# A masked-patch loss on one core: identities ahead of the loads, target loads further forward, last columns divided over two engine paths

## Chip, cores, metric

One core of one Trainium2 chip. The metric is the device time of one execution in microseconds. "Span" is the time from the first to the last instruction in the profile of one execution; the metric is some 1.7 us more.

## The reference

```python
# pred, target: (32, 147, 768) float32; norm_pix_loss = True
mean = target.mean(axis=-1, keepdims=True)
var = target.var(axis=-1, keepdims=True)
target = (target - mean) / np.sqrt(var + 1e-6)
loss = np.mean((pred - target) ** 2, axis=-1)
return loss.mean(axis=-1)          # 32 numbers
```

## The kernel before

The 32 x 147 rows lie on 128 partitions as 36 full "columns" of 128 rows and one REST column of 96 rows, each 768 wide. One column is 0.393 MB in f32; pred and target are 28.90 MB together. Each column goes through five steps:

- VectorE takes mean and variance (two `bn_stats`, one `bn_aggr`);
- ScalarE and VectorE make 1/sqrt(var) for a group of columns;
- GpSimd normalises the column to bf16 (`s`);
- the difference pred - s is formed either on TensorE (two products with identities, accumulated in tiles in PSUM, whose size the code counts in banks; called the ACT path) or on VectorE (`difference`);
- the square with its sum along the row is taken on ScalarE or VectorE, and at the end TensorE adds the partial sums over partitions in `acc`.

The first target columns and REST are loaded as f32 by SyncE's and ScalarE's queues; all else is loaded by GpSimd's queue, which casts to bf16 on the way.

```python
    piece("t", 0, 4, q="hw")                   # SyncE's queue, f32
    piece("t", REST, REST + 1, q="hw2")        # ScalarE's queue, f32
    piece("t", 4, 8)                           # GpSimd's queue, cast to bf16
    piece("p", REST, REST + 1)
    piece("t", 8, 12)
    piece("p", 0, 4)
    ...
    piece("t", 28, 32)
    piece("p", 12, 16)
    piece("t", 32, 36)
    for c in range(16, 32, 2):
        piece("p", c, c + 2)
    for c in range(32, 35):
        piece("p", c, c + 1)
    piece("p", KM - 1, KM, 0, half)
    piece("p", KM - 1, KM, half, D)
    ...
    units = [((c, c + 1), 0, D, "ACT" if c < 18 else "DVE+ACT") for c in range(0, 24, 2)]
    units.insert(2, ((REST,), 0, D, "ACT"))
    units += [((24,), 0, D, "DVE"), ((25,), 0, D, "DVE+ACT"), ((26, 27), 0, D, "DVE+ACT")]
    units += [((c,), 0, D, "ACT" if c % 2 else "DVE") for c in range(28, KM - 1)]
    units += [((KM - 1,), 0, half, "ACT"), ((KM - 1,), half, D, "ACT")]
```

Every operation gets an assumed duration, its needs, a rank and an earliest time. A small list scheduler in the kernel's own source (not on the chip) emits them in the order in which this model would start them. On the chip each engine then works **in that order**, whether or not something behind is ready earlier (below, VectorE stands idle for 1.29 us with ready work behind).

```python
            t = max([free[engine], early] + [end[x] + (0.0 if ops[by_name[x]][1] == engine else HOP) for x in needs])
            key = (t - (1.0 if name[0] == "root" else 0.0), rank, i)
```

GpSimd has eight load slots in this kernel: its load k is issued only after its load k - 8 has landed (before: the first landed at 11.78 us, the ninth was issued at 12.06).

Of the kernel before, what the change touches and what calls it, by code (L numbers as in the profile page):

```python
# [7 lines left out]
F32 = mybir.dt.float32  # L8
# [6 lines left out]
def kernel(  # L15
# [26 lines left out]

    data = ctx.enter_context(tc.tile_pool(name="data", bufs=1))
    work = ctx.enter_context(tc.tile_pool(name="work", bufs=16))
    diffs = ctx.enter_context(tc.tile_pool(name="diffs", bufs=4))
    small = ctx.enter_context(tc.tile_pool(name="small", bufs=8))
    singles = ctx.enter_context(tc.tile_pool(name="singles", bufs=1))
    psum = ctx.enter_context(tc.tile_pool(name="psum", bufs=2, space=bass.MemoryType.PSUM))
    psum1 = ctx.enter_context(tc.tile_pool(name="psum1", bufs=1, space=bass.MemoryType.PSUM))


# [3 lines left out]
    def piece(kind, c0, c1, d0=0, d1=D, q="sw"):  # L55
        stream.append((kind, c0, c1, d0, d1, q))

    piece("t", 0, 4, q="hw")
    piece("t", REST, REST + 1, q="hw2")
    piece("t", 4, 8)  # L60
    piece("p", REST, REST + 1)
    piece("t", 8, 12)
    piece("p", 0, 4)
    piece("t", 12, 16)
    piece("t", 16, 20)
    piece("p", 4, 8)
    piece("t", 20, 24)
    piece("t", 24, 28)
    piece("p", 8, 12)
    piece("t", 28, 32)  # L70
    piece("p", 12, 16)
    piece("t", 32, 36)
    for c in range(16, 32, 2):
        piece("p", c, c + 2)
    for c in range(32, 35):
        piece("p", c, c + 1)
# [1 line left out]
    piece("p", KM - 1, KM, half, D)  # L78


    groups = [tuple(range(0, 4)), (REST,)] + [tuple(range(c, c + 4)) for c in range(4, 16, 4)]
    groups += [(c, c + 1) for c in range(16, KM, 2)]


    units = [((c, c + 1), 0, D, "ACT" if c < 18 else "DVE+ACT") for c in range(0, 24, 2)]
    units.insert(2, ((REST,), 0, D, "ACT"))
    units += [((24,), 0, D, "DVE"), ((25,), 0, D, "DVE+ACT"), ((26, 27), 0, D, "DVE+ACT")]
    units += [((c,), 0, D, "ACT" if c % 2 else "DVE") for c in range(28, KM - 1)]
    units += [((KM - 1,), 0, half, "ACT"), ((KM - 1,), half, D, "ACT")]



# [3 lines left out]
    def op(name, engine, dur, needs, fn, rank=0.0, early=0.0):  # L96
        by_name[name] = len(ops)
        ops.append((name, engine, dur, needs, fn, rank, early))
# [13 lines left out]
            KIND[kind].setdefault(c, []).append((d0, d1, til, (c - c0) * w))  # L112


    land, lanes, clock = {}, {"hw": [], "hw2": [], "sw": []}, 2.9
    for i, (kind, c0, c1, d0, d1, q) in enumerate(stream):
        w = (c1 - c0) * (d1 - d0)
        clock += w * rows_of(c0) / P * 0.915 / D + (0.0 if w >= 4 * D else 0.04)
# [7 lines left out]
    def landed(kind, c):  # L126
        return max(t for (k, cc, d), t in land.items() if k == kind and cc == c)
# [19 lines left out]
                                        base=per - 1, pattern=[[per, B]], channel_multiplier=-1))  # L147

    op("eps", "DVE", 0.1, [], lambda: pin(nc.vector.memset(eps_t, eps)))
    op("ident", "POOL", 1.6, [], identities, early=2.0)  # L150
    op("masks", "POOL", 3.0, [], masks, early=3.0)

    mvs = {}
# [9 lines left out]
    def stats(g, i):  # L163
        n, K = rows_of(g[0]), len(g)
        if i == 0:
            mvs[g] = small.tile([P, K, 2], F32, name="mv")
        if not norm_pix_loss:
            return
        (_, _, til, o), = tbuf[g[i]]
        bn(mvs[g][:n, i], [til[:n, o + a:o + a + half] for a in (0, half)])  # L170
# [20 lines left out]

    for k, g in enumerate(groups):
        for i, c in enumerate(g):
            op(("bn", c), "DVE", 1.26, [], lambda g=g, i=i: stats(g, i), rank=k - 50.0, early=landed("t", c))
        op(("root", k), "ACT", 0.55, [("bn", c) for c in g], lambda g=g: root(g), rank=-1.0)
        op(("recip", k), "DVE", 0.2, [("root", k)], lambda g=g: recip(g), rank=-60.0)

# [21 lines left out]

    def product(u, d0, w, src, so, eye, first):  # L220
        n, z = rows_of(u[0]), zs[u, d0]
        for a in range(0, w, BANK):
            b = min(w, a + BANK)
            pin(nc.tensor.matmul(z[:n, a:b], eye[:n, :n], src[:n, so + a:so + b], start=first, stop=not first))  # L224

    def sub_target(u, d0, w):
        if (u, d0) == units[-1][:2]:
            zs[u, d0] = psum1.tile([P, BANK], F32, name="z_last")
        else:
            zs[u, d0] = psum.tile([P, 3 * BANK], F32, name="z")  # L230
        s, so = sbuf[u[0]]
        product(u, d0, w, s, so + d0, nident, True)

# [7 lines left out]
    def difference(u, d0, w):  # L241

        z = zs[u, d0] = diffs.tile([P, 2 * D], BF16, name="zd")
        s, so = sbuf[u[0]]
        til, o = pred_of(u[0], d0)
        pin(nc.vector.tensor_tensor(out=z[:, :w], in0=til[:, o:o + w], in1=s[:, so + d0:so + d0 + w],  # L246
                                    op=ALU.subtract))

    def square_dve(u, d0, w, dest):
        z = zs[u, d0][:, :w]  # L250
        pin(nc.vector.scalar_tensor_tensor(out=z, in0=z, scalar=1.0, in1=z, op0=ALU.mult, op1=ALU.mult,  # L251
                                           accum_out=dest))

    tail = 5
    n_early = len(units) - 1 - tail
    rl = singles.tile([P, n_early], F32)
    rl_sum = singles.tile([P, 1], F32)
    finals = []
    early_ops, users, seen = [], [], set()
    for k, (u, d0, d1, eng) in enumerate(units):  # L260
        w = len(u) * D if len(u) > 1 else d1 - d0
        arrive = max(t for (kk, c, d), t in land.items() if kk == "p" and c in u and d < d1)
        norms = [("norm", c) for c in u]
        for c in u:
# [11 lines left out]
            dest = singles.tile([P, 1], F32, name=f"rl{k}")  # L276
            finals.append((("sq", k), dest, mask, P))
        if eng in ("DVE", "DVE+ACT"):
            op(("diff", k), "DVE", 0.57 * w / D + 0.05, norms, lambda u=u, d0=d0, w=w: difference(u, d0, w), rank=-2.0,
               early=arrive)  # L280
            if eng == "DVE":
                op(("sq", k), "DVE", 1.0 * w / D, [("diff", k)],
                   lambda u=u, d0=d0, w=w, dest=dest: square_dve(u, d0, w, dest), rank=-1.0)
            else:
                op(("sq", k), "ACT", 0.75 * w / D + 0.25, [("diff", k)],
                   lambda u=u, d0=d0, w=w, dest=dest: square_act(u, d0, w, dest), rank=k)
            continue
        op(("subt", k), "PE", 0.37 * w / D, norms + (users[-2:-1] if k < len(units) - 1 else []) + ["ident"],
           lambda u=u, d0=d0, w=w: sub_target(u, d0, w), rank=k + 0.0)
        op(("pred", k), "PE", 0.37 * w / D, [("subt", k)], lambda u=u, d0=d0, w=w: add_pred(u, d0, w), rank=k,  # L290
           early=arrive)
        op(("sq", k), "ACT", 0.73 * w / D + 0.23, [("pred", k)],
           lambda u=u, d0=d0, w=w, dest=dest: square_act(u, d0, w, dest), rank=k)
        users.append(("sq", k))

    acc = psum1.tile([1, B], F32)
    def early_sum():
        junk = singles.tile([P, n_early], F32, name="junk")
        pin(nc.scalar.activation(out=junk, in_=rl, func=ACTF.Copy, accum_out=rl_sum))

    op("rl_sum", "ACT", 0.4, early_ops, early_sum, rank=50.0)
    finals.insert(0, ("rl_sum", rl_sum, mask, P))
    turn = []

    def final(vec, m, n):
        turn.append(n)
        pin(nc.tensor.matmul(acc, vec[:n], m[:n], start=len(turn) == 1, stop=len(turn) == len(finals)))  # L307

    for i, (need, vec, m, n) in enumerate(finals):
        op(("final", i), "PE", 0.2, [need, "masks"], lambda v=vec, m=m, n=n: final(v, m, n), rank=90.0)  # L310


    HOP = 0.15
# [59 lines left out]
```

## Time and profile before

| | before |
|---|---|
| time, median | 77.22 us (3 runs, 77.22 to 77.61) |
| span | 75.4 us |
| first data packet / last landing | 2.20 / 71.50 us |
| copy of the result to SBUF, then its transfer | 73.26 us |
| busy: VectorE, GpSimd, ScalarE, TensorE | 75, 72, 42, 40% |

The prediction shows the page's lines for these. How to read them: in the 40-slice rows a digit is the busy share of one slice in tenths. In a window's row each engine has its busy time and (x instructions), and the last three columns are TensorE's granted clock, DMA share and GB/s written. In a timeline's row stand start, duration, engine, line, operation and tiles, and in brackets how long the engine had been idle and who released it. "Landing" is the last of the completion records of a load.

### The profile page before, as it was taken

The page shows a single profiled execution, that of the slowest core. Times are in us where ns is not written, and L with a number is a line of the kernel's source. Part 1 is how long each engine was busy: PE and PEld are TensorE (multiplying, and loading weights), DVE is VectorE, ACT ScalarE, POOL GpSimd, SP SyncE. Part 2 cuts the span into 40 slices and gives each one's busy share as a digit, 9 for nine tenths or more (in the row PEclk, how much of TensorE's full clock was granted, in tenths as well). Part 3 has the DMA queues.
Part 4 walks back from the last instruction along what each step waited for, and adds up shares of the span by engine and source line. Part 5 has one row for each costly group of instructions (what it writes and reads, how often), then busy time and mean ns, then how long its engine had stood idle before and what let it go on. Part 6 is the DMA issues. An engine that isn't in the chain of part 4 may idle for free.

```text
span 75.4 us, 570 instructions
## 1 busy us (share of the span) xinstructions
PE 30.3 (40%) x87; PEld 8.7 (11%) x88; DVE 56.3 (75%) x148; ACT 32.0 (42%) x73; POOL 54.4 (72%) x77
## 2 busy tenths in 40 slices
PE   0000000038596540688700778287544000348860
PEld 0000000001232110211100211031111000112220
DVE  0000099999999999976999928960999989989940
ACT  1400000210229802289210297239366099799550
POOL 4998205099999999499989898999878799800000
PEclk9999999999999997555555557965995555555555
DMA  0899999999999999999999999999999999999700
GB/s 0 215 424 339 262 192 236 218 209 215 212 215 215 212 216 225 212 209 215 215 212 215 219 212 225 209 212 202 214 215 209 215 210 210 214 205 205 117 0 0
DMA packets 3973, 15.41 MB, mean 204 GB/s; under 512 B 450, under 2 KB 1186, under 8 KB 3842
## 3 DMA queue, kind: packets, MB, share of 16 engines
q0 software_dynamic: 3712, 13.52, 89.2%
q1 hardware_dynamic: 146, 1.57, 5.7%
q10 hardware_dynamic: 112, 0.29, 1.0%
q14 instruction: 3, 0.02, 0.1%
HBM read 28.90 MB, written 0.00 MB: 383 GB/s over the span
## 4 chain that ended last, share of the span: by engine, by line
DMA 60%; DVE 18%; POOL 9%; issue 6%; PE 2%; ACT 1%; POOLq 0%; ACTq 0%
DMA t<-in_target_dram 49%; DVE st L160 14%; DMA p<-in_pred_dram 11%; POOL s L210 8%; DVE mv L161 3%; DVE zd L246 1%; PE acc L307 1%; POOL t L110 1%; PE z L224 1%; ACT z_last L239 1%; PE z_last L224 1%; POOLq L368 0%; DVE r L190 0%; POOL p L110 0%; DVE ob L336 0%
## 5 line engine op out<-in xcount | busy, mean ns | idle before, releaser
L160 DVE BATCH_NORM_STATS2 st<-t 128x6 f32<-128x384 bf16 (+2 forms) x74 | 36.3, 532 | 11.6 <-DMA t<-in_target_dram 11.6
L210 POOL TENSOR_SCALAR s<-t,nm,r 128x768 bf16<-128x768 bf16 (+2 forms) x37 | 38.2, 1040 | 3.2 <-ACT nm L185 2.0
L224 PE MATMUL z<-s,nident 128*128 128x512 bf16 (+4 forms) x36 | 14.6, 511 | 23.3 <-POOL s L210 17.6
L239 ACT ACTIVATE z<-z 128x1536 f32<-128x1536 f32 (+3 forms) x14 | 16.6, 1184 | 6.9 <-PE z L224 6.8
L224 PE MATMUL z<-p,ident 128*128 128x512 bf16 (+4 forms) x35 | 14.2, 542 | 12.1 <-DMA p<-in_pred_dram 12.0
L184 ACT ACTIVATE r<-mv,eps_t 128x2 f32<-128x2 f32 (+2 forms) x15 | 4.4, 293 | 29.5 <-DVE mv L161 28.8
L110 POOL DMA_DIRECT2D p<-in_pred_dram x18 | 10.2, 565 | 2.7 <-DVE st L160 1.0
L246 DVE TENSOR_TENSOR zd<-p,s 128x768 bf16<-128x768 bf16 (+1 forms) x10 | 9.7, 991 | 0.5 <-ACT zd L239 0.3
L161 DVE BATCH_NORM_AGGREGATE mv<-st 128x2 f32<-128x12 f32 (+1 forms) x37 | 7.7, 209 | 1.3
L110 POOL DMA_DIRECT2D t<-in_target_dram x8 | 4.9, 628 | 4.7 <-DMA t<-in_target_dram 3.9
L239 ACT ACTIVATE zd<-zd 128x1536 bf16<-128x1536 bf16 (+1 forms) x5 | 6.7, 1345 | 2.7 <-DVE zd L246 2.7
L224 PEld LDWEIGHTS <-ident 128*128 128x128 bf16 (+1 forms) x37 | 4.7, 126 | 27.2 <-issue 26.2
L224 PEld LDWEIGHTS <-nident 128*128 128x128 bf16 (+1 forms) x37 | 3.4, 114 | 34.6 <-issue 14.4
L251 DVE SCALAR_TENSOR_TENSOR zd<-zd 128x768 bf16<-128x768 bf16 x5 | 4.8, 955 | 0.1
L224 PE MATMUL z_last<-s,nident 128*128 128x384 bf16 x1 | 0.5, 479 | 7.1 <-POOL s L210 7.1
L190 DVE RECIPROCAL r<-r 128x2 f32<-128x2 f32 (+2 forms) x15 | 1.9, 123 | 1.7 <-ACT r L184 1.7
L185 ACT ACTIVATE nm<-mv 128x2 f32<-128x2 f32 (+2 forms) x15 | 2.8, 188 | 0.0
L239 ACT ACTIVATION_READ_ACCUMULATOR z<-z 128x1 f32 (+1 forms) x14 | 2.7, 190 | 0.0
L184 ACT ACT_TABLE_LOAD x1 | 1.3, 1283 | 1.5 <-PEq L354 1.5
L307 PE MATMUL acc<-mask,rl 128*1 128x32 f32 x10 | 1.0, 224 | 0.4 <-ACT z_last L239 0.4
L239 ACT ACTIVATION_READ_ACCUMULATOR zd<-zd 128x1 f32 x5 | 0.9, 187 | 0.0
L336 DVE COPY ob<-acc 1x32 f32<-1x32 f32 x1 | 0.2, 178 | 1.0 <-PE acc L307 1.0
(26 smaller groups left out, 5.8 us busy)
## 6 DMA issues: line engine op xcount, KB each, us to landing
t<-in_target_dram POOLq DMA_DIRECT2D x8, 768.0 KB, 24.5
p<-in_pred_dram POOLq DMA_DIRECT2D x4, 768.0 KB, 27.4
p<-in_pred_dram POOLq DMA_DIRECT2D x8, 384.0 KB, 20.9
t<-in_target_dram SPq DMA_DIRECT2D x1, 1536.0 KB, 8.4
p<-in_pred_dram POOLq DMA_DIRECT2D x3, 192.0 KB, 12.7
t<-in_target_dram ACTq DMA_DIRECT2D x1, 288.0 KB, 9.6
p<-in_pred_dram POOLq DMA_DIRECT2D x2, 96.0 KB, 7.3
p<-in_pred_dram POOLq DMA_DIRECT2D x1, 144.0 KB, 10.4
```

The costliest lines, as they stand in the source:

```text
L110: pin(eng.dma_start(out=til[:n], in_=src))
L160: pin(nc.vector.bn_stats(out=st[:n, j, :], in_=x))
L161: pin(nc.vector.bn_aggr(out=out, in_=st[:n, :len(parts)]))
L184: pin(nc.scalar.activation(out=r[:n], in_=mv[:n, :, 1], func=ACTF.Sqrt, bias=eps_t[:n], scale=1.0))
L185: pin(nc.scalar.activation(out=nm[:n], in_=mv[:n, :, 0], func=ACTF.Copy, scale=-1.0))
L190: pin(nc.vector.reciprocal(out=rs[g][:n], in_=rs[g][:n]))
L210: pin(nc.gpsimd.tensor_scalar(out=s[:n, so:so + D], in0=til[:n, o:o + D], scalar1=nm, scalar2=r, op0=ALU.add, op1=ALU.mult))
L224: pin(nc.tensor.matmul(z[:n, a:b], eye[:n, :n], src[:n, so + a:so + b], start=first, stop=not first))
L239: pin(nc.scalar.activation(out=z[:n, :w], in_=z[:n, :w], func=ACTF.Square, accum_out=dest[:n]))
L246: pin(nc.vector.tensor_tensor(out=z[:, :w], in0=til[:, o:o + w], in1=s[:, so + d0:so + d0 + w], op=ALU.subtract))
L251: pin(nc.vector.scalar_tensor_tensor(out=z, in0=z, scalar=1.0, in1=z, op0=ALU.mult, op1=ALU.mult, accum_out=dest))
L307: pin(nc.tensor.matmul(acc, vec[:n], m[:n], start=len(turn) == 1, stop=len(turn) == len(finals)))
```

## The change

The intent is to make the identities while no data are there yet, to let target run further ahead of pred so that statistics and normalisation are done earlier, to make groups and pieces of four columns, and to divide the last columns so that ScalarE and VectorE each take a part of every one.

```diff
+    piece("t", 8, 12)
     piece("p", REST, REST + 1)
-    piece("t", 8, 12)
+    piece("t", 12, 16)
     piece("p", 0, 4)
-    piece("t", 12, 16)
 ... (each target piece moved forward likewise)
     piece("p", 8, 12)
-    piece("t", 28, 32)
-    piece("p", 12, 16)
     piece("t", 32, 36)
-    for c in range(16, 32, 2):
+    for c in range(12, 24, 4):
+        piece("p", c, c + 4)
+    for c in range(24, 32, 2):
         piece("p", c, c + 2)
 ...
+    groups = [(0, 1), (2, 3), (REST,)] + [tuple(range(c, c + 4)) for c in range(4, KM, 4)]
+    units = [((c, c + 1), 0, D, "ACT" if c < 14 else "DVE+ACT") for c in range(0, 24, 2)]
+    units += [((24,), 0, D, "DVE"), ((25,), 0, D, "DVE+ACT")]
+    for u in [(c, c + 1) for c in range(26, KM - 4, 2)] + [(c,) for c in range(KM - 4, KM - 1)]:
+        m = BANK if u[0] < KM - 2 else half
+        units += [(u, 0, m, "ACT"), (u, m, D, "DVE")]
+    units += [((KM - 1,), 0, half, "ACT"), ((KM - 1,), half, D, "DVE")]
 ...
-    op("ident", "POOL", 1.6, [], identities, early=2.0)
+    op("ident", "POOL", 1.3, [], identities, rank=-2.0)
 ...
-            op(("bn", c), ..., rank=k - 50.0, early=landed("t", c))
+            op(("bn", c), ..., rank=k - 50.0 if c < 32 or c == REST else -1.5, early=landed("t", c))
```

With it come two pools of accumulators in turn (two of three banks for the pairs, then three of two banks, `zp`, for the tail), five difference buffers for four, the sum of the early parts on VectorE instead of ScalarE, and new durations in the scheduler's model. The REST column was on ScalarE's queue already, so that part of the description changes nothing.

More of the change, by code (lines that the diff above doesn't have):

```diff
@@ L44 @@
     work = ctx.enter_context(tc.tile_pool(name="work", bufs=16))
-    diffs = ctx.enter_context(tc.tile_pool(name="diffs", bufs=4))
+    diffs = ctx.enter_context(tc.tile_pool(name="diffs", bufs=5))
     small = ctx.enter_context(tc.tile_pool(name="small", bufs=8))
     singles = ctx.enter_context(tc.tile_pool(name="singles", bufs=1))
-    psum = ctx.enter_context(tc.tile_pool(name="psum", bufs=2, space=bass.MemoryType.PSUM))
     psum1 = ctx.enter_context(tc.tile_pool(name="psum1", bufs=1, space=bass.MemoryType.PSUM))
@@ L60 @@
     piece("t", 4, 8)
+    piece("t", 8, 12)
     piece("p", REST, REST + 1)
-    piece("t", 8, 12)
+    piece("t", 12, 16)
     piece("p", 0, 4)
-    piece("t", 12, 16)
     piece("t", 16, 20)
+    piece("t", 20, 24)
     piece("p", 4, 8)
-    piece("t", 20, 24)
     piece("t", 24, 28)
+    piece("t", 28, 32)
     piece("p", 8, 12)
-    piece("t", 28, 32)
-    piece("p", 12, 16)
     piece("t", 32, 36)
-    for c in range(16, 32, 2):
+    for c in range(12, 24, 4):
+        piece("p", c, c + 4)
+    for c in range(24, 32, 2):
         piece("p", c, c + 2)
@@ L78 @@
     piece("p", KM - 1, KM, half, D)
-    groups = [tuple(range(0, 4)), (REST,)] + [tuple(range(c, c + 4)) for c in range(4, 16, 4)]
-    groups += [(c, c + 1) for c in range(16, KM, 2)]
-    units = [((c, c + 1), 0, D, "ACT" if c < 18 else "DVE+ACT") for c in range(0, 24, 2)]
+    groups = [(0, 1), (2, 3), (REST,)] + [tuple(range(c, c + 4)) for c in range(4, KM, 4)]
+    units = [((c, c + 1), 0, D, "ACT" if c < 14 else "DVE+ACT") for c in range(0, 24, 2)]
     units.insert(2, ((REST,), 0, D, "ACT"))
-    units += [((24,), 0, D, "DVE"), ((25,), 0, D, "DVE+ACT"), ((26, 27), 0, D, "DVE+ACT")]
-    units += [((c,), 0, D, "ACT" if c % 2 else "DVE") for c in range(28, KM - 1)]
-    units += [((KM - 1,), 0, half, "ACT"), ((KM - 1,), half, D, "ACT")]
+    units += [((24,), 0, D, "DVE"), ((25,), 0, D, "DVE+ACT")]
[3 more added lines that the diff above has]
+    units += [((KM - 1,), 0, half, "ACT"), ((KM - 1,), half, D, "DVE")]
     ops, by_name = [], {}
@@ L112, in load @@
             KIND[kind].setdefault(c, []).append((d0, d1, til, (c - c0) * w))
-    land, lanes, clock = {}, {"hw": [], "hw2": [], "sw": []}, 2.9
+    land, lanes, clock = {}, {"hw": [], "hw2": [], "sw": []}, 2.3
     for i, (kind, c0, c1, d0, d1, q) in enumerate(stream):
@@ L193 @@
         for i, c in enumerate(g):
-            op(("bn", c), "DVE", 1.26, [], lambda g=g, i=i: stats(g, i), rank=k - 50.0, early=landed("t", c))
+            op(("bn", c), "DVE", 1.26, [], lambda g=g, i=i: stats(g, i), rank=k - 50.0 if c < 32 or c == REST else -1.5, early=landed("t", c))
         op(("root", k), "ACT", 0.55, [("bn", c) for c in g], lambda g=g: root(g), rank=-1.0)
@@ L221, in product @@
         n, z = rows_of(u[0]), zs[u, d0]
-        for a in range(0, w, BANK):
-            b = min(w, a + BANK)
-            pin(nc.tensor.matmul(z[:n, a:b], eye[:n, :n], src[:n, so + a:so + b], start=first, stop=not first))
+        runs = [(0, so, w)] if w % D == 0 else [(k * BANK, so + k * D, w // len(u)) for k in range(len(u))]
+        for zo, o, e in runs:
+            for a in range(0, e, BANK):
+                b = min(e, a + BANK)
+                pin(nc.tensor.matmul(z[:n, zo + a:zo + b], eye[:n, :n], src[:n, o + a:o + b],
+                                     start=first, stop=not first))
     def sub_target(u, d0, w):
-        if (u, d0) == units[-1][:2]:
-            zs[u, d0] = psum1.tile([P, BANK], F32, name="z_last")
-        else:
-            zs[u, d0] = psum.tile([P, 3 * BANK], F32, name="z")
+        if u in pairs_pe:
+            zs[u, d0] = pools["pairs"].tile([P, 3 * BANK], F32, name="z")
+            pairs_pe.remove(u)
+        else:
+            if "parts" not in pools:
+                pools["stack"].close()
+                pools["parts"] = ctx.enter_context(tc.tile_pool(name="parts", bufs=3, space=bass.MemoryType.PSUM))
+            zs[u, d0] = pools["parts"].tile([P, 2 * BANK], F32, name="zp")
         s, so = sbuf[u[0]]
@@ L245, in difference @@
         til, o = pred_of(u[0], d0)
-        pin(nc.vector.tensor_tensor(out=z[:, :w], in0=til[:, o:o + w], in1=s[:, so + d0:so + d0 + w],
-                                    op=ALU.subtract))
+        K, e = len(u), w // len(u)
+        if e == D:
+            x, y, v = z[:, :w], til[:, o:o + w], s[:, so:so + w]
+        elif K == 1:
+            x, y, v = z[:, :w], til[:, o:o + w], s[:, so + d0:so + d0 + w]
+        else:
+            x = z[:, :w].rearrange("p (k d) -> p k d", d=e)
+            y = til[:, o - d0:o - d0 + K * D].rearrange("p (k d) -> p k d", d=D)[:, :, d0:d0 + e]
+            v = s[:, so:so + K * D].rearrange("p (k d) -> p k d", d=D)[:, :, d0:d0 + e]
+        pin(nc.vector.tensor_tensor(out=x, in0=y, in1=v, op=ALU.subtract))
     def square_dve(u, d0, w, dest):
@@ L252, in square_dve @@
                                            accum_out=dest))
-    tail = 5
+    tail = 6
     n_early = len(units) - 1 - tail
@@ L257 @@
     rl_sum = singles.tile([P, 1], F32)
+    pairs_pe = [u for u, d0, d1, eng in units if eng == "ACT" and (u[0] == REST or len(u) * (d1 - d0) > 2 * BANK)]
+    n_pairs = len(pairs_pe)
+    pools = {"stack": ExitStack()}
+    pools["pairs"] = pools["stack"].enter_context(tc.tile_pool(name="psum", bufs=2, space=bass.MemoryType.PSUM))
     finals = []
-    early_ops, users, seen = [], [], set()
+    early_ops, users, dusers, dprev, seen = [], [], [], [], set()
     for k, (u, d0, d1, eng) in enumerate(units):
-        w = len(u) * D if len(u) > 1 else d1 - d0
+        w = len(u) * (d1 - d0)
         arrive = max(t for (kk, c, d), t in land.items() if kk == "p" and c in u and d < d1)
@@ L278 @@
         if eng in ("DVE", "DVE+ACT"):
-            op(("diff", k), "DVE", 0.57 * w / D + 0.05, norms, lambda u=u, d0=d0, w=w: difference(u, d0, w), rank=-2.0,
+            op(("diff", k), "DVE", 0.57 * w / D + 0.05, norms + dusers[-5:-4] + dprev[-1:], lambda u=u, d0=d0, w=w: difference(u, d0, w), rank=-2.0,
                early=arrive)
+            dusers.append(("sq", k))
+            dprev.append(("diff", k))
             if eng == "DVE":
@@ L284 @@
             else:
-                op(("sq", k), "ACT", 0.75 * w / D + 0.25, [("diff", k)],
+                op(("sq", k), "ACT", 0.65 * w / D + 0.22, [("diff", k)],
                    lambda u=u, d0=d0, w=w, dest=dest: square_act(u, d0, w, dest), rank=k)
             continue
-        op(("subt", k), "PE", 0.37 * w / D, norms + (users[-2:-1] if k < len(units) - 1 else []) + ["ident"],
+        op(("subt", k), "PE", 0.37 * w / D, norms + (users[-2:-1] if len(users) < n_pairs else users[n_pairs - 1:n_pairs] + users[n_pairs:][-3:-2]) + ["ident"],
            lambda u=u, d0=d0, w=w: sub_target(u, d0, w), rank=k + 0.0)
@@ L291 @@
            early=arrive)
-        op(("sq", k), "ACT", 0.73 * w / D + 0.23, [("pred", k)],
+        op(("sq", k), "ACT", 0.65 * w / D + 0.22, [("pred", k)],
            lambda u=u, d0=d0, w=w, dest=dest: square_act(u, d0, w, dest), rank=k)
@@ L296 @@
     acc = psum1.tile([1, B], F32)
-    def early_sum():
-        junk = singles.tile([P, n_early], F32, name="junk")
-        pin(nc.scalar.activation(out=junk, in_=rl, func=ACTF.Copy, accum_out=rl_sum))
-    op("rl_sum", "ACT", 0.4, early_ops, early_sum, rank=50.0)
+    op("rl_sum", "DVE", 0.2, early_ops, lambda: pin(nc.vector.tensor_reduce(
+        out=rl_sum, in_=rl, axis=mybir.AxisListType.X, op=ALU.add)), rank=-3.0)
     finals.insert(0, ("rl_sum", rl_sum, mask, P))
@@ L309 @@
     for i, (need, vec, m, n) in enumerate(finals):
-        op(("final", i), "PE", 0.2, [need, "masks"], lambda v=vec, m=m, n=n: final(v, m, n), rank=90.0)
+        op(("final", i), "PE", 0.2, [need, "masks"], lambda v=vec, m=m, n=n: final(v, m, n), rank=90.0,
+           early=max(land.values()) + 0.4)
     HOP = 0.15
```

## The prediction

> **What bounds the kernel now.** I read the page first: the slices of part 2 (is anything full all the time?), then part 4 (the chain that ended last), then windows and timelines of the first 12 us and the last 15 us. From the page:
>
> ```profile
> span 75.4 us, 570 instructions
> PE 30.3 (40%) x87; PEld 8.7 (11%) x88; DVE 56.3 (75%) x148; ACT 32.0 (42%) x73; POOL 54.4 (72%) x77
> ...
> DMA  0899999999999999999999999999999999999700
> GB/s 0 215 424 339 262 192 236 218 209 215 212 215 215 212 216 225 212 209 215 215 212 215 219 212 225 209 212 202 214 215 209 215 210 210 214 205 205 117 0 0
> ...
> DMA 60%; DVE 18%; POOL 9%; issue 6%; PE 2%; ACT 1%; POOLq 0%; ACTq 0%
> ```
>
> The reader is to see that no engine is full but the transfers are: the DMA row holds a 9 from slice 2 (3.8 us) to slice 36 (69.7 us). The kernel reads 28.90 MB, a fixed amount, and the loads by GpSimd write half of what they read (f32 to bf16), so 215 GB/s written is 430 GB/s read. The windows of the stretches give the rates:
>
> ```profile
> 12.00:40.00 28.00, 13.60 (x36) 3.85 (x36) 26.20 (x79) 10.10 (x28) 24.18 (x29) 0.81 1.04 215
> 52.00:60.00 8.00, 3.40 (x10) 0.83 (x9) 7.17 (x15) 3.81 (x9) 6.92 (x9) 0.71 1.07 210
> 60.00:66.00 6.00, 0.66 (x2) 0.21 (x2) 5.77 (x10) 5.33 (x8) 5.26 (x4) 0.50 1.08 212
> 66.00:70.00 4.00, 2.75 (x8) 0.91 (x7) 3.63 (x9) 3.61 (x8) 0.00 (x0) 0.50 1.12 204
> ```
>
> The last two columns are DMA share and GB/s: full everywhere, 2% slower with two-column pieces (from about 52 us), 5% with the smallest at the end. So the time has three parts: a head until the engines are full (first data packet at 2.20 us by the packet records, full from 3.5 us), a body of transfers until the last piece has landed (71.50 us by the landing records; the piece before it 71.00), and a tail of 3.9 us to the end of the span. The tail, from the timeline:
>
> ```profile
> 71.05 0.48 PE L224 MATMUL z<-p,ident 128*128 128x384 bf16 x1 [0.26 <-DMA p<-in_pred_dram]
> 71.30 0.96 DVE L251 SCALAR_TENSOR_TENSOR zd<-zd 128x768 bf16<-128x768 bf16 x1
> ...
> 71.78 0.50 PE L224 MATMUL z_last<-p,ident 128*128 128x384 bf16 x1
> ...
> 72.32 0.47 ACT L239 ACTIVATE z_last<-z_last 128x384 f32<-128x384 f32 x1 [0.18 <-PE z_last L224]
> 72.71 0.19 ACT L239 ACTIVATION_READ_ACCUMULATOR z_last<-z_last 128x1 f32 x1
> ...
> 72.96 0.26 PE L307 MATMUL acc<-mask,rl 128*1 128x32 f32 x2 [0.37 <-ACT z_last L239]
> 73.26 0.18 DVE L336 COPY ob<-acc 1x32 f32<-1x32 f32 x1 [0.99 <-PE acc L307]
> ```
>
> The last half column (z_last) lands at 71.50, but PE is busy with accumulations until 71.78, then PE, ScalarE and PE again: its sum is ready at 72.90. VectorE is nearly as late: its square of column 34 ends at 72.26. From the copy to the end of the span there are 2.1 us (the output's transfer), which nothing here changes.
>
> **What the Trainium skill says.** "DMA: Bandwidth & Descriptors", section "Where 436 GB/s comes from", puts the ceiling of a core's ports at 435 GB/s; the trace agrees, 430 GB/s read in the body. So nothing that makes an engine faster can shorten the body. The same page, section "Issuing engines are not separate DMA queues", says that loads issued by different engines interleave on the same 16 DMA engines; the trace agrees: from 5 to 8 us packets of all three queues alternate. Its specifications give about 1 us to the first byte of a GpSimd load; the trace differs: GpSimd issues its first at 1.32 and its first packet moves at 5.78, 4.46 us later, behind the f32 load. "GPSIMD Engine Reference", section "Key points", says that GpSimd shares its SBUF interfaces with VectorE, with contention for VectorE instructions with two SBUF inputs. The trace shows it: the difference zd<-p,s of 1536 elements takes 0.90 to 0.95 us where two ran back to back, but 2.69 us at 57.45 while GpSimd normalises, and a normalisation (0.98 usually) takes 2.29 us at 60.42 during two differences.
>
> **The change part by part.**
> (a) Identities first. In the timeline they run at 5.64 to 6.93, 1.29 us. Ahead of the loads they put GpSimd's first issue off by 0.8 to 1.3 us (to 2.1 to 2.6), and by the same 4.46 us its first packet to 6.6 to 7.05. Do the DMA engines run dry? By 5.5 us 93 of the 128 big f32 packets and 13 of the 96 of the REST column have started. Left are 35 x 0.473 + 83 x 0.121 = 26.6 us of one engine, / 16 = 1.66 us, so that work lasts until 7.16. Just enough: cost 0, at worst 0.3 us. In return the first four target columns no longer share with GpSimd's load and land some 1.2 us earlier (before: 9.23).
> (b) The REST column on ScalarE's queue: the kernel before already loads it so. Nothing.
> (c) Target further forward. Columns 32 to 35 are behind 49.5 columns of stream, not 53.5; a column costs 0.916 us here (0.393 MB / 0.429), so they land 3.7 us earlier: 49.1 for 52.80. Their statistics (1.13 us a column on VectorE, from the chain: 0.90 + 0.21 + 0.02) end at about 53.5 for 57.3, and GpSimd's last normalisation near 59 for 65.2. It moves no bytes and so no end of the body by itself: it makes slack for VectorE's last 15 us.
> (d) Pred 16 to 24 in pieces of four columns: 3.15 MB at 429 rather than 420 GB/s, 7.33 for 7.50 us: the body ends 0.17 us earlier, last landing 71.33. Two issues fewer on GpSimd (0.56 each) lie beside.
> (e) Groups of four for root: 11 for 15, four times 0.48 us off ScalarE and 0.12 off VectorE, beside.
> (f) Pairs 14 and 16 to the VectorE path: +2 x 0.95 us there. The later units are split: VectorE gets 512 columns of each pair 26, 28, 30, 256 of 32 and 33, 384 of 34 and 35. With 0.145 + w/1920 us for a difference (0.545 at 768), 0.157 + w/960 for the square (0.957 at 768) and 0.08 for the sum's read: 1.18, 0.78 and 0.98 us. Five pair differences 4.7, column 24 1.6, column 25 0.55, three pairs 3.5, two columns 1.6, two halves 2.0: 13.9 us between 53.5 and the end, where it has 17.8 until 71.33. Up to 4 us of contention with GpSimd's last four normalisations still fit, so VectorE should keep up with the landings.
> (g) The end. Second half of 35 lands at 71.33; difference 0.35, square 0.56, read 0.08: 72.35. First half lands at 70.83; PE 0.48, then ScalarE, which is finishing 34 until 71.45: + 0.58 = 72.05. ScalarE backwards: pair 30 lands 67.47, two products 0.86, square of 1024 at 1.0 + 0.1, then 0.68 each for 32 and 33 and 0.6 for 34; that fits. So the last partial sum is there at 72.35 for 72.90: 0.55 us, of which 0.17 are of (d).
> Sum: 0 (a, most likely) - 0.55 (d and g) = 76.67; with a little of (a)'s risk, 76.7 us.
>
> **The rivals.** (1) A hole at the start: GpSimd's loads come 1.3 us later, and every idle us of the DMA engines is a us of the time. For it: the margin in (a) is 0.1 to 0.5 us. Against: 4.46 us is probably partly a wait behind f32 packets, which would not grow. It would give 76.9 to 77.3. (2) VectorE as the bound at the end: it was back to back from 57 to 72 and gets more differences, which lock against GpSimd. For it: the 2.69 us above. Against: 3.7 us of head start. If it ended 1 us late, 77.5. (3) Everything is hidden: body and output transfer are the same, and the gain of the split is eaten by accumulations on PE (eight now, seven before) or by ScalarE: 77.2, no difference. (4) A larger gain would need a shorter body; the only idle capacity is the ramp from 2.2 to 3.5 us (0.7 us at most), and no part touches it.
>
> **Range and chances.** The certain parts are small: 67 of 77 us are bytes at the ceiling. From 76.2 (all gains and a cleaner start) to 77.3 (hole at the start, tail as before). Faster by over 2% means below 75.68, 1.5 us, nearly all of the tail that is not output: chance 0.05. Slower by over 2%, above 78.8, needs a hole over 1.5 us or VectorE 2 us late: 0.03. Within 2%: 0.92.
>
> **What would show it.** (a) right: the identities at about 1 us, first GpSimd packets at 6.6 to 7.1, no slice under 9 in slices 2 to 4, first landing near 8. (c) right: the last statistics end near 53.5, GpSimd's last normalisation before 61. (d) right: the last landing at 71.3 +- 0.3. (g) right: the last VectorE square within 1.1 us of that landing and the last accumulation near 72.4. I am wrong if a slice of the DMA row dips, if the last square starts more than 0.3 us behind its difference, or if the chain at the end runs back through VectorE or GpSimd rather than to the landing.

## The result and the profile after

The changed kernel took **77.03 us** (median of 6 runs, 76.89 to 77.14) against 77.24 us for the kernel before (6 runs): ratio 0.9962, 95% interval 0.9942 to 0.9983. The difference is small and real, and the verdict at 2% is "same".

The page of the changed kernel, its span, engines, transfers and chain:

```profile
span 75.3 us, 551 instructions
PE 30.0 (40%) x81; PEld 8.8 (12%) x82; DVE 56.2 (75%) x155; ACT 30.4 (40%) x65; POOL 53.5 (71%) x75
...
DMA  0899999999999999999999999999999999999700
...
DMA 40%; DVE 34%; POOL 12%; ACT 3%; PE 3%; issue 3%; ACTq 0%; POOLq 0%
```

The DMA row is the same, digit for digit. The chain is put together differently in the middle, but the end of the body is not: the last landing is at 71.54 us, for 71.50 before. What moved is the tail, in the changed kernel's timeline:

```profile
71.63 0.36 DVE L265 TENSOR_TENSOR zd<-p,s 128x384 bf16<-128x384 bf16 x1
...
72.03 0.56 DVE L269 SCALAR_TENSOR_TENSOR zd<-zd 128x384 bf16<-128x384 bf16 x1
72.11 0.48 ACT L249 ACTIVATE zp<-zp 128x384 f32<-128x384 f32 x1
72.51 0.08 DVE L269 DVE_READ_ACCUMULATOR zd<-zd 128x1 f32 x1
72.51 0.19 ACT L249 ACTIVATION_READ_ACCUMULATOR zp<-zp 128x1 f32 x1
...
73.16 0.18 DVE L359 COPY ob<-acc 1x32 f32<-1x32 f32 x1 [0.57 <-PE acc L328]
```

The two halves of column 35 now end side by side, VectorE's at 72.59 and ScalarE's at 72.70, where ScalarE's last ended at 72.90. The copy comes 1.62 us after the last landing instead of 1.76.

The rest of the profile shows that the forward order worked only half. Target 32 to 36 landed at 49.27, for 52.80. But VectorE's timeline of the changed kernel has this:

```profile
51.54 0.21 DVE L162 BATCH_NORM_AGGREGATE mv<-st 128x2 f32<-128x12 f32 x1
53.04 0.96 DVE L265 TENSOR_TENSOR zd<-p,s 128x1536 bf16<-128x1536 bf16 x1 [1.29 <-DMA p<-in_pred_dram]
53.91 1.01 DVE L161 BATCH_NORM_STATS2 st<-t 128x6 f32<-128x384 bf16 x2
```

After two of the last four columns VectorE stands idle for 1.29 us in front of a difference whose pred has not landed, with the statistics of columns 34 and 35 ready behind it. The scheduler's model had that pred landed by then and put the difference first: of operations that could start at the same time the lower rank goes first, and here -2.0 stands against -1.5, the rank that this change itself gave to the last statistics. So the statistics ended at 56.3 us and GpSimd's last normalisation at 65.5, no earlier than before (65.2).

### The profile page after: what moved, and what is told of

It is laid out like the page before. It is cut to its first block, busy times and chain, and to the rows that moved or that the text cites. A ratio compares the mean times of both kernels' runs of the same rounds, so it can differ in the third digit from the quotient of the medians. Undisturbed runs are those within 1.5% of the kernel's fastest.

```text
span 75.3 us, 551 instructions
## 1 busy us (share of the span) xinstructions
PE 30.0 (40%) x81; PEld 8.8 (12%) x82; DVE 56.2 (75%) x155; ACT 30.4 (40%) x65; POOL 53.5 (71%) x75
## 4 chain that ended last, share of the span: by engine, by line
DMA 40%; DVE 34%; POOL 12%; ACT 3%; PE 3%; issue 3%; ACTq 0%; POOLq 0%
DMA p<-in_pred_dram 29%; DVE st L161 28%; DMA t<-in_target_dram 11%; POOL s L211 11%; DVE mv L162 6%; ACT zp L249 3%; PE zp L228 3%; POOL p L111 1%; PE acc L328 1%; DVE r L191 0%; ACTq L391 0%; DVE ob L359 0%; ACTq L249 0%; POOLq L211 0%
## 5 line engine op out<-in xcount | busy, mean ns | idle before, releaser
L228 PE MATMUL z<-p,ident 128*128 128x512 bf16 (+2 forms) x23 | 10.4, 616 | 17.6 <-DMA p<-in_pred_dram 17.6
L228 PE MATMUL z<-s,nident 128*128 128x512 bf16 (+2 forms) x23 | 10.1, 563 | 16.6 <-POOL s L211 15.4
L249 ACT ACTIVATE z<-z 128x1536 f32<-128x1536 f32 (+1 forms) x8 | 10.9, 1357 | 10.6 <-PE z L228 10.6
L185 ACT ACTIVATE r<-mv,eps_t 128x4 f32<-128x4 f32 (+2 forms) x11 | 3.2, 292 | 27.7 <-DVE mv L162 27.0
L265 DVE TENSOR_TENSOR zd<-p,s 128x1536 bf16<-128x1536 bf16 (+4 forms) x14 | 9.6, 700 | 3.6 <-DMA p<-in_pred_dram 3.5
L228 PE MATMUL zp<-p,ident 128*128 128x512 bf16 (+1 forms) x9 | 4.7, 594 | 6.9 <-DMA p<-in_pred_dram 6.9
L249 ACT ACTIVATE zp<-zp 128x1024 f32<-128x1024 f32 (+2 forms) x7 | 5.1, 735 | 1.8 <-PE zp L228 1.8
L228 PE MATMUL zp<-s,nident 128*128 128x512 bf16 (+1 forms) x10 | 5.0, 607 | 2.0 <-ACT z L249 1.7
L269 DVE SCALAR_TENSOR_TENSOR zd<-zd 128x512 bf16<-128x512 bf16 (+3 forms) x8 | 5.0, 623 | 0.2
L186 ACT ACTIVATE nm<-mv 128x4 f32<-128x4 f32 (+2 forms) x11 | 2.1, 190 | 0.0
```

The lines of the kernel that those rows point to most:

```text
L185: pin(nc.scalar.activation(out=r[:n], in_=mv[:n, :, 1], func=ACTF.Sqrt, bias=eps_t[:n], scale=1.0))
L186: pin(nc.scalar.activation(out=nm[:n], in_=mv[:n, :, 0], func=ACTF.Copy, scale=-1.0))
L228: pin(nc.tensor.matmul(z[:n, zo + a:zo + b], eye[:n, :n], src[:n, o + a:o + b], start=first, stop=not first))
L249: pin(nc.scalar.activation(out=z[:n, :w], in_=z[:n, :w], func=ACTF.Square, accum_out=dest[:n]))
L265: pin(nc.vector.tensor_tensor(out=x, in0=y, in1=v, op=ALU.subtract))
L269: pin(nc.vector.scalar_tensor_tensor(out=z, in0=z, scalar=1.0, in1=z, op0=ALU.mult, op1=ALU.mult, accum_out=dest))
```

## The experiments

The theory after the result: bytes set the end of the body, the gain is the shorter tail, and part of the predicted tail was lost to a wait for an accumulator. The rivals: a poorer start through the identities; the order of the loads as the true source, through VectorE's head start; differences that are only scatter. Kernels are compared only within the same rounds.

| run | median us (range) | ratio to before, 95% | last landing | landing to copy |
|---|---|---|---|---|
| changed kernel | 77.03 (76.89 to 77.14) | 0.9962 (0.9942, 0.9983) | 71.54 | 1.62 |
| own_banks | 76.88 (76.73 to 77.09) | 0.9966 (0.9954, 0.9978) | 71.60 | 1.41 |
| ident_back | 76.90 (76.74 to 76.96) | 0.9964 (0.9952, 0.9976) | 71.43 | 1.62 |
| two_col | 77.44 (76.94 to 77.65) | 1.0031 (1.0007, 1.0056) | 71.52 | 2.03 |
| tail_only | 77.14 (76.96 to 77.53) | 1.0005 (0.9986, 1.0024) | 71.63 | 1.60 |
| after_again | 76.95 (76.75 to 77.14) | 0.9975 (0.9959, 0.9992) | 71.43 | 1.51 |
| own_banks2 | 76.89 (76.78 to 77.11) | 0.9972 (0.9958, 0.9986) | 71.41 | 1.50 |
| best | 77.02 (76.95 to 77.10) | 0.9985 (0.9973, 0.9997) | 71.46 | 1.67 |
| order_back | 78.28 (78.02 to 78.38) | 1.0143 (1.0126, 1.0160) | 71.35 | 2.80 |
| before_again | 77.21 (1 run) | - | 71.58 | 1.75 |
| masks_first | 77.10 (77.06 to 77.34) | 0.9984 (0.9970, 0.9997) | 71.95 | 1.52 |
| order_back_stats | 76.87 (76.60 to 77.02) | 0.9950 (0.9933, 0.9968) | 71.52 | 1.36 |
| no_p12 (wrong) | 74.77 (74.73 to 74.87) | 0.9685 (0.9670, 0.9700) | 67.89 | 3.05 |

Each row has 4 to 6 executions, before_again one. The kernel before had medians of 77.15, 77.11 and 77.23 us in the three calls. The last two columns are from one profile each. Two profiles of one kernel differ by up to 0.18 us in the landing and up to 0.12 us in the stretch to the copy, which is the limit of what can be read from them.

### own_banks and own_banks2: the wait for an accumulator

In the changed kernel's timeline TensorE, at 69.96 us, starts the product for column 34 only when ScalarE has freed an accumulator, and the ready product of column 33 stands behind it. ScalarE is then idle for 0.48 us.

```profile
69.96 0.50 PE L228 MATMUL zp<-s,nident 128*128 128x384 bf16 x1 [0.35 <-ACT zp L249]
...
70.99 0.58 ACT L249 ACTIVATE zp<-zp 128x512 f32<-128x512 f32 x1 [0.48 <-PE zp L228]
```

```diff
-                pools["parts"] = ctx.enter_context(tc.tile_pool(name="parts", bufs=3, ...))
-            zs[u, d0] = pools["parts"].tile([P, 2 * BANK], F32, name="zp")
+                for nb, bufs in ((2, 2), (1, 3)):      # 2 tiles of two banks, 3 of one bank
+                    pools[nb] = ctx.enter_context(tc.tile_pool(name=f"parts{nb}", bufs=bufs, ...))
+            zs[u, d0] = pools[len(u)].tile([P, len(u) * BANK], F32, name=...)
 (and the needs of the products in the scheduler's model to match)
```

> The changed kernel, but the accumulator tiles of the tail are two of two banks (pairs 26, 28, 30) and three of one bank (columns 32, 33, 34, first half of 35) instead of three of two banks. Theory (the predicted 0.55 us shrank because TensorE, in order, held the ready product of column 33 behind the product of column 34, which waited until 69.96 us for a free accumulator): ScalarE's idle 0.48 us before 70.99 goes, its last square ends near 72.2 for 72.70, VectorE's last sum (72.59) becomes the last one, the copy of the result moves from 73.16 to about 72.95, time 0.15 to 0.25 us below the changed kernel's 77.03: 76.8 to 76.9. Rival (the landing and VectorE alone set the end): no change, 77.03 within 0.07.

> The kernel with the accumulator tiles of one bank for the single columns, a second time, now beside the changed kernel. Theory (TensorE held ScalarE up by a wait for an accumulator): copy 1.4 us after the last landing instead of 1.6, time 0.15 to 0.25 us below after_again of the same rounds. Rival (times differ by where the last landing falls, and the tail's 0.2 us are within that scatter): no difference clear of the interval.

The wait of 0.48 us went, though in own_banks2 a later one of 0.31 us took part of its place: ScalarE's last sum came 0.69 us (own_banks) and 1.05 us (own_banks2) after the last landing, instead of 1.16 and 1.14 in the two profiles of the changed kernel. The time did not follow. Beside the changed kernel on one chip it was 76.89 against 76.95, ratios 0.9972 against 0.9975, the same. VectorE's last sum, at 72.65 and 72.47 us, had taken over. The wait was real and worth nothing measurable, so the theory that it had eaten a measurable part of the gain fell.

### ident_back: identities behind the loads

```diff
-    op("ident", "POOL", 1.3, [], identities, rank=-2.0)
+    op("ident", "POOL", 1.6, [], identities, early=2.0)
```

> The changed kernel with the identities back behind the first eight loads of GpSimd. Theory (the engines never run dry at the start, so the identities' place is free): first GpSimd packet back from 5.97 to 5.78 us, last landing unchanged at 71.54 within 0.1, time 77.03 within 0.08. Rival (the later loads cost a hole or a poorer start, which hides the gain of the larger pieces): last landing 0.15 to 0.2 us earlier, time 76.85.

The first GpSimd packet moved back to 5.69 us, the last landing was 71.43 (the changed kernel: 71.54 and 71.43), and the ratio 0.9964 is between the changed kernel's 0.9962 and 0.9975. The place of the identities is worth nothing that these runs can measure, in either direction.

### masks_first: how much later may GpSimd's loads start?

```diff
-    op("masks", "POOL", 3.0, [], masks, early=3.0)
+    op("masks", "POOL", 1.5, [], masks, rank=-2.0)
```

> The changed kernel with the masks ahead of the loads of GpSimd as well, so that its first load is issued near 3.1 us instead of 1.83. Theory (the first GpSimd packet waits behind f32 packets already queued, so it moves by less than the issue does, and the engines do not run dry before 7.2 us): first packet at 6.3 to 6.9 us, DMA share full throughout, last landing within 0.1 us of 71.5, time within 0.1 us of the changed kernel, 76.85 to 77.05. Rival (a fixed 4.1 us from issue to packet): first packet at 7.2 us, some hole, time 0.1 to 0.3 us more, 77.1 to 77.3.

The timeline of this run, GpSimd alone, shows the first load behind both:

```profile
1.60 0.29 POOL L139 TENSOR_SCALAR_AFFINE_SELECT nident<-nident 128x128 bf16<-128x128 bf16 x1
...
2.93 0.21 POOL L147 TENSOR_SCALAR_AFFINE_SELECT mask_rest<-mask_rest 96x32 f32<-96x32 f32 x1
3.08 1.24 POOL L111 DMA_DIRECT2D t<-in_target_dram  x2
```

The first packet came at 7.16 us, 4.08 after the issue, as the rival said. In the ten profiles with an issue at 1.83 us or later it came 3.9 to 4.2 us after the issue; in the four with an issue at 1.32 it came 4.4 to 4.6 us after, at 5.69 to 5.87, so something held those. What, is open. The first four target columns landed at 8.90 us (9.08 to 9.33 in the profiles with an issue at 1.83 or 1.84): the mechanism of the prediction's step (a) exists, but it needs a later GpSimd load.

The rival's hole is there too. While the first packet was awaited, the DMA share fell, here from 6 to 7.2 us beside the same stretch of the changed kernel (second row):

```profile
6.00:7.20 1.20, 0.00 (x0) 0.00 (x0) 0.00 (x0) 0.00 (x0) 1.20 (x3) 1.00 0.87 300
```

```profile
6.00:7.20 1.20, 0.00 (x0) 0.00 (x0) 0.00 (x0) 0.00 (x0) 0.99 (x6) 1.00 0.98 317
```

That is 0.13 us of 16 engines. What it cost in time is not settled. The last landing of this profile (71.95) is 0.4 to 0.5 us later than the changed kernel's, but the profiled execution was the slowest of the six (77.34 us; the other five took 77.06 to 77.13). The ratio 0.9984 is 0.1 to 0.2% above the changed kernel's two, and its interval overlaps both of theirs.

### two_col: pieces of two columns for pred 16 to 24

```diff
-    for c in range(12, 24, 4):
-        piece("p", c, c + 4)
-    for c in range(24, 32, 2):
+    piece("p", 12, 16)
+    for c in range(16, 32, 2):
         piece("p", c, c + 2)
```

> The changed kernel with pred 16 to 24 in four pieces of two columns, as before the change. Theory (the larger pieces do save what the packet times say, and something else in the body took it back): the 8 columns take 7.48 instead of 7.35 us, last landing 0.13 to 0.17 us later, time 77.15 to 77.2. Rival (the size of the pieces is worth nothing): 77.03 within 0.07.

The eight columns took 7.42 us (landings 52.83 to 60.25) instead of 7.35, and the last landing was 71.52. So the pieces are worth 0.07 us here (0.13 between the first profiles of before and after, 7.48 to 7.35). Yet the kernel was slower than expected and scattered over 0.7 us. The reason was elsewhere, in its timeline:

```profile
65.19 2.72 DVE L268 SCALAR_TENSOR_TENSOR zd<-zd 128x512 bf16<-128x512 bf16 x1
```

```profile
65.44 1.94 POOL L210 TENSOR_SCALAR s<-t,nm,r 128x768 bf16<-128x768 bf16 x2
```

This square takes 0.69 us elsewhere. It lasted through both of GpSimd's last normalisations, and VectorE carried the delay to the end: its last sum came at 73.23, for 72.59. Why these normalisations ran so late is in VectorE's timeline before that:

```profile
56.82 1.53 DVE L264 TENSOR_TENSOR zd<-p,s 128x1536 bf16<-128x1536 bf16 x1
58.28 1.00 DVE L160 BATCH_NORM_STATS2 st<-t 128x6 f32<-128x384 bf16 x2
...
60.56 0.18 DVE L190 RECIPROCAL r<-r 128x4 f32<-128x4 f32 x1 [0.20 <-ACT r L184]
```

With the new pieces the scheduler put the last two statistics behind one and two more differences than in the changed kernel. They ended at 59.53 us, for 56.29, and the last group's reciprocal came at 60.56, for 57.74. This is the fault that order_back shows below. So this run tests the size of the pieces by its landings alone, and its time says nothing of them.

### tail_only: the division of the last columns alone

```diff
 (against the changed kernel: loads, groups, identities and the limit c < 18 of the kernel before;
  division of the last columns, pools and sum on VectorE kept; statistics always first in rank)
```

> The kernel before with the division of the last columns over two paths alone (with its accumulator pools and the sum of the early parts on VectorE); order and size of the loads, groups, identities and path of pairs 14 and 16 as before. Theory (the gain of 0.2 us is all in the tail, the loads' order is worth nothing by itself): time 77.0 to 77.15, copy of the result near 73.15. Rival (the division needs the head start that the order of the loads gives VectorE; without it VectorE, with its 4 statistics at 53 to 57 us, ends late): 77.2 or more, with a VectorE backlog: its last square begins more than 0.5 us after the last landing.

Landing to copy was 1.60 us, as in the changed kernel, but the last landing in this profile was 71.63, and the ratio of the times 1.0005 (0.9986 to 1.0024). The tail got shorter, and no gain in time is shown. This run is inconclusive for the split of a gain of 0.2 us: it is as large as the interval. That the tail is the source of the changed kernel's gain therefore rests on the profiles (landing to copy), not on this time.

### order_back: the loads in the old order

```diff
 (against the changed kernel: the stream of the kernel before, with pred 16 to 24 in pieces of four columns)
```

> The changed kernel with the loads in the order of the kernel before (target columns 32 to 36 behind pred 12 to 16), pieces of the same sizes. Theory (the order only makes slack on VectorE and GpSimd): target 32 to 36 lands at 52.9 instead of 49.3, the last landing and the copy do not move, time within 0.1 us of after_again. Rival (VectorE's head start is what lets the division of the tail work): VectorE's last squares begin late, time 0.3 us or more above after_again.

This was the largest effect: 78.28 us, 1.7% slower than after_again by the ratios (1.0143 against 0.9975). The rival was right. The bytes landed as before (71.35), but VectorE was late. Its timeline and GpSimd's:

```profile
56.50 2.11 DVE L266 TENSOR_TENSOR zd<-p,s 128x1536 bf16<-128x1536 bf16 x2 [0.21 <-DMA p<-in_pred_dram]
58.54 1.00 DVE L162 BATCH_NORM_STATS2 st<-t 128x6 f32<-128x384 bf16 x2
...
61.06 0.17 DVE L192 RECIPROCAL r<-r 128x4 f32<-128x4 f32 x1
...
63.90 3.13 DVE L266 TENSOR_TENSOR zd<-p,s 128x512 bf16<-128x512 bf16 x1 [0.20 <-DMA p<-in_pred_dram]
...
73.27 0.56 DVE L270 SCALAR_TENSOR_TENSOR zd<-zd 128x384 bf16<-128x384 bf16 x1
```

```profile
61.43 1.86 POOL L212 TENSOR_SCALAR s<-t,nm,r 128x768 bf16<-128x768 bf16 x1 [0.53 <-DVE r L192]
63.25 0.56 POOL L112 DMA_DIRECT2D p<-in_pred_dram  x1
63.86 2.90 POOL L212 TENSOR_SCALAR s<-t,nm,r 128x768 bf16<-128x768 bf16 x3
```

The statistics of the last column stand behind two differences of pred and run at 58.54. So the last group's reciprocal comes at 61.06 and GpSimd's last three normalisations run from 63.86 to 66.76. They hold the difference of 512 columns, 0.42 us elsewhere, for 3.13 us: it starts 0.04 us after the first of the three does and ends 0.27 us after the last has ended, so it waited for all of them. From 66.96 on VectorE never waits again, and it is 1.2 us late at the end.

### order_back_stats: the old order, but statistics first

```diff
 (against order_back)
-            op(("bn", c), ..., rank=k - 50.0 if c < 32 or c == REST else -1.5, ...)
+            op(("bn", c), ..., rank=k - 50.0, ...)
```

> The run with the loads in the old order (78.28 us, VectorE late from 64 us on), with one thing more: the statistics of the last four target columns ahead of all differences in VectorE's order. Theory (there the last statistics stood behind differences that waited for pred, so the last group's root came at 61 us, GpSimd normalised its last columns from 61.4 to 66.8 us and locked VectorE's difference of pair 26 out for 3.1 us, and that backlog reached the end): statistics done near 57.5, last normalisation done by 64 us, no difference longer than 2 us after 63, the copy 1.5 to 1.7 us after the last landing, time back to 77.0 to 77.15. Rival (the old order costs the time by itself, through VectorE's total work after 52.8 us): still 77.8 or more.

One rank gave the 1.4 us back: **76.87 us**, ratio 0.9950. The statistics ended at 57.6 us and the reciprocal came at 58.34, 2.7 us earlier:

```profile
57.51 0.91 DVE L266 TENSOR_TENSOR zd<-p,s 128x1536 bf16<-128x1536 bf16 x1
58.34 0.17 DVE L192 RECIPROCAL r<-r 128x4 f32<-128x4 f32 x1
...
65.54 1.38 DVE L270 SCALAR_TENSOR_TENSOR zd<-zd 128x512 bf16<-128x512 bf16 x1
```

Two details of the expectation missed: GpSimd's last normalisation ended at 66.4 us, not by 64 (beside VectorE's differences and squares three of the last four took 1.48, 2.28 and 1.81 us, for 0.97), and the landing to the copy took 1.36 us, less than 1.5. But now the last normalisations came one at a time, and the longest hold after 65 us was 1.38 us for 0.69, which VectorE recovered before 69.7 us. So the old order costs nothing by itself. It costs some 1.3 us only together with the rank that puts the last statistics behind the differences. This kernel has the lowest ratio of all, but its interval (0.9933 to 0.9968) overlaps the changed kernel's two, so it is not shown to beat it. It was run at another time.

### best: everything that looked good, together

```diff
 (one-bank tiles as own_banks; statistics first as above; and)
-    for c in range(12, 24, 4):
+    for c in range(12, 28, 4):
         piece("p", c, c + 4)
```

> One-bank tiles for the single columns, pred 24 to 28 as one piece of four columns, and the statistics of the last four target columns ahead of all differences in VectorE's order. Theory (bytes and the tail set the time): last landing 0.05 to 0.08 us earlier by the larger piece, tail as own_banks, time 0.2 to 0.3 us below after_again. Rival (the pieces that land together leave ScalarE or VectorE late in the tail): copy more than 1.5 us after the last landing, no gain over own_banks2.

A miss. The copy came 1.67 us after the landing and the ratio was 0.9985, no better than after_again's 0.9975: columns 24 to 28 now land together, at 63.89 (VectorE waits 1.29 us for them), and VectorE is still finishing column 34 at 71.8 when the last half has landed (71.46). The rival was right. But three things were changed at once, so that the piece is to blame is argued, not shown. The run shows something else: statistics first in rank ended at 53.96 us, and GpSimd still ended at 65.03, because the last group's reciprocal stood behind a difference that was held for 3.63 us (0.96 alone), and GpSimd's normalisations were held in turn (three took 5.69 us, for 2.9):

```profile
53.88 3.63 DVE L268 TENSOR_TENSOR zd<-p,s 128x1536 bf16<-128x1536 bf16 x1
57.42 0.16 DVE L191 RECIPROCAL r<-r 128x4 f32<-128x4 f32 x1
```

```profile
57.80 5.69 POOL L211 TENSOR_SCALAR s<-t,nm,r 128x768 bf16<-128x768 bf16 x3 [0.41 <-DVE r L191]
```

### no_p12: how much room is there under the bytes?

```diff
+        if (kind, c0) == ("p", 12):            # wrong on purpose: not loaded, 8 to 12 used twice
+            for c in range(c0, c1):
+                pbuf[c] = pbuf[c - 4]
+            return
```

> Wrong result on purpose: the changed kernel without the load of pred 12 to 16 (1.57 MB read; columns 8 to 12 are used twice), all instructions of the engines the same. Theory (bytes bind the body, every byte taken away comes off at the rate of the body): last landing 3.66 us earlier, near 67.85, and the time 3.3 to 3.7 us below the changed kernel, 73.2 to 73.6, if VectorE, which has 3.5 us of waits for pred to give, just keeps up. Rival (VectorE or GpSimd bind nearly as hard): last landing as early, but VectorE late in the tail, time 74 us or more.

The last landing came 3.65 us earlier (67.89 for 71.54), as the bytes say, but the time fell by only 2.4 us against the kernel before (74.77 for 77.23), some 2.2 against the changed kernel. The copy came 3.05 us after the landing. VectorE had become the bound, with GpSimd at its side; GpSimd's row here is two normalisations (1.94 us when left alone):

```profile
56.19 4.22 DVE L269 TENSOR_TENSOR zd<-p,s 128x1536 bf16<-128x1536 bf16 x5
```

```profile
56.48 5.49 POOL L215 TENSOR_SCALAR s<-t,nm,r 128x768 bf16<-128x768 bf16 x2 [0.60 <-DVE r L195]
```

So bytes do bind the changed kernel, and VectorE together with GpSimd comes only about 2 us behind. (The record has this result as correct: the check of the loss does not notice four columns used twice.)

### before_again: scatter

> The kernel before once more, for a second profile of it: how far do the last landing (71.50 us in the first profile) and the stretch from it to the copy of the result (1.76 us) move from run to run? Theory (the gain is in the tail): the stretch stays 1.7 to 1.8 us, while the changed kernel showed 1.62 and 1.51. Rival (the two differ only by scatter): 1.6 us or less here.

The last landing was 71.58 (first profile 71.50), and landing to copy 1.75 us. The tail of the kernel before is 1.76 and 1.75 and that of the changed kernel 1.62 and 1.51; ident_back, tail_only and masks_first, with the same tail, have 1.62, 1.60 and 1.52. The shortening by 0.13 to 0.25 us is not scatter.

## Why the prediction was right

The time (77.03 for 76.7 predicted) lay within the range, and "within 2%" was right for the reason given: the bytes fill the span and no part of the change touches them. The gain itself was 0.2 to 0.3 us where 0.55 were predicted. Of its steps:

- **The bound.** Right, and shown by no_p12: a load taken away moves the last landing by its bytes. One reading needs a limit: the 435 GB/s that the prediction cites is a ceiling of the ports into SBUF, and of the 430 GB/s read only 215 were written there. That the transfers were full is shown; that these ports filled them is not. But the prediction gave VectorE too much room. Its rival (2) was closer than it looked: order_back lost 1.2 us to it, no_p12 about 1.5.
- **(a) Identities.** "Cost 0" was right (ident_back), but not because the margin held: it was never needed. The identities put only 1.02 us in front of the issue, not 1.29, and began at 0.81, in a gap in which GpSimd had been idle until 1.32, so the issue moved by 0.51 us and the packet only from 5.78 to 5.97, not to 6.6 to 7.05. For that reason the step that failed is "the first four target columns ... land some 1.2 us earlier": they landed at 9.27, for 9.23. masks_first, with the packet at 7.16, shows the effect at 0.2 to 0.4 us. It also shows that the sum "that work lasts until 7.16" was too generous: there the DMA share was down to 0.87 from 6 to 7.2 us.
- **(c) Target further forward.** The landing was right (49.27 for 49.1). "Their statistics end at about 53.5" and "GpSimd's last normalisation near 59" failed: 56.3 and 65.5. What the prediction left out is that each engine works in the order the kernel's scheduler emits. The difference of pair 14 stood in front of the statistics and waited for pred. For the normalisations this is not the whole: in best the statistics ended at 53.96 and the last normalisation still at 65.03. The prediction's 59 priced the normalisations alone, without what VectorE's differences and they take from each other.
- **(d) Larger pieces.** The term was 0.17 us and measured 0.07 to 0.13. The last landing is no evidence: 71.33 was predicted, and 71.54 and 71.43 came, for 71.50 and 71.58 before; the scatter is as large as the term.
- **(f) VectorE keeps up.** Right for the changed kernel. The formula for the square, which the kernel before shows at one width only, came out: 0.69, 0.56 and 0.42 us at 512, 384 and 256. The waits for pred are 3.5 us in all:

```profile
DVE zd L265 <- DMA p<-in_pred_dram: 3.5, 4, 1.6
```

- **(g) The end.** The mechanism was right. From the last landing to VectorE's last sum 1.02 us were predicted and 1.05 measured, in both profiles. Two terms were mis-sized. ScalarE's last sum came 1.16 and 1.14 us after that landing instead of 0.72, because TensorE waited for an accumulator; own_banks shows that this did not matter. And after the last sum the accumulation took 0.46 and 0.37 us to the copy, where the prediction took over 0.36 from the kernel before. So the sum of 0.55 us became 0.2 to 0.3 in the time: (d) lost in scatter, and 0.13 to 0.25 us from the tail, as the profiles have it.
- **Rival (3)**, "the gain of the split is eaten by accumulations on PE", held for 0.1 us of it in one profile and 0.01 in the other.

## What to carry to other kernels

When the transfers are full from head to tail, price a change by the last landing and by what follows it, and expect no more. But look at the runner-up too: an engine order that lets an early stage (here the last statistics) stand behind a late one can push two engines that share an interface into each other, and then a reordering of loads that is harmless by itself costs 1.3 us. See to it that operations that feed other engines do not wait behind ones that need later data, and test the parts of a change one at a time: here the later rank of the statistics did no measurable harm in the changed kernel, but with the old order of the loads it made a kernel slower than either (order_back), and two_col's timeline shows it again with nothing but other pieces.

## What the Trainium skill lacked or had wrong

- "DMA: Bandwidth & Descriptors", section "Specifications", gives about 1 us to the first byte of a load from GpSimd. Here it took 3.9 to 4.2 us from the issue to the first packet at the start of a kernel (issue 1.83, packet 5.97; issue 3.08, packet 7.16), and 4.4 to 4.6 us for issues at 1.32. The page does not say how it changes when f32 loads of other queues are in front.
- "SBUF — State Buffer", section "Who interferes with whom", says that the pair of ports that VectorE and GpSimd share is an exclusive lock: who issues first has it for the whole instruction, and the other is blocked. The runs agree that one blocks the other. What the page lacks is who gets the lock next when instructions follow each other closely. It was not always the one that waited: a VectorE difference of 0.42 us lasted 3.13 us, through three GpSimd normalisations of 0.97 to 0.98 us, and a square of 0.69 us lasted 2.72, through two; two normalisations of 1.94 us together took 5.49 us beside a run of differences. In other places it was: in best a difference begun at 60.33 us had ended at 61.85, in spite of normalisations from 60.07 to 63.49 without a gap. No run here shows the rule; a schedule has to allow for a whole run of the other engine's instructions, not for one.
